# Three pairs of gate/up chunks per FFN in seven block products for both token tiles, with normed rows and an explicit order of steps

## The chip, the core and the metric

One NeuronCore of a Trainium2 chip runs the whole program. The metric is the device time of one execution in microseconds (us), lower is better; the median of the runs of a kernel is compared. Five engines work side by side, each through its own queue in order: the tensor engine (PE; its weight loads are shown apart as PEld), the vector engine (DVE), the scalar engine (ACT), GpSimd (POOL) and the sync engine (SP), which here only issues transfers (DMAs).

## The reference

Two layers, each of three sublayers, on 256 tokens of width 1024 in float32:

```
x = x + 0.5 * rms_norm(swiglu(rms_norm(x, g1), wg, wu, wd), g1post)      # FFN 1
x = x + rms_norm(hybrid_mixer(rms_norm(x, gm), ...), gmpost)             # three attentions, gated
x = x + 0.5 * rms_norm(swiglu(rms_norm(x, g2), wg, wu, wd), g2post)      # FFN 2

def swiglu(x, wg, wu, wd):
    return (jax.nn.silu(x @ wg) * (x @ wu)) @ wd                         # 1024 -> 2816 -> 1024
```

The change is in the four FFNs, in how their weights are prepared, and in what sets the order; the mixers compute as before.

## The kernel before, in words

**Tiles.** The tokens are two tiles of 128, called lanes 0 and 1. All weights lie in one array as 212 half-blocks of 128 x 2048 float32 (1 MB), in the order of their use. An FFN has 11 chunks of 256 columns; a chunk has two half-blocks of gate and up columns side by side (512 columns, four slices of K each) and one half-block for the product down (two slices of K, 1024 columns). An FFN is 33 half-blocks, a mixer 40.

**Precision.** The products run in float32r. `Stream.split` (L74 to L92) makes two float32r parts of each weight, a quarter-block of 128 x 1024 at a time: ACT copies it to `whi` (L88), DVE subtracts to get `wlo` (L89). The inputs are transposed on PE and split likewise (`split_T`, L192 to L199). `mm3` (L240) then takes three matmuls for one product: hi by hi (L245), hi by lo (L247), lo by hi (L250). A half-block with one lane is so 12 matmuls of 512 columns, called a block product here, whether it is of gate/up, of down, or of the mixer.

**Order.** Each lane is a generator that yields after a block product; a list of places (L625 to L645) runs lane 1 `LAG` = 3 half-blocks behind lane 0, so that each half-block of split weights serves both. Six split half-blocks (`W_BUFS`) and three unsplit ones (`RAW_BUFS`) fit. The framework then schedules the traced instructions into one queue for each engine.

**Between sublayers.** `postnorm` (L223) sums the squares of the down product on ACT (L163), takes the power on POOL (L155, L157), scales on DVE (L232) and adds to the residual `x` (L233). `gained` (L207, L211) multiplies by the next gain only, `prenorm` (L213) transposes that (L197), and the reciprocal of the norm is applied later, as a scale of the rows that come out of the products (L303, L305). So PE can begin with a sublayer before its norm is known. Both lanes do this, one about three half-blocks after the other, while PE works for the other lane.

**Names.** In the kernel before, `f010` is layer 0, second FFN, lane 0, and `f011` its lane 1; `m01` is the mixer of layer 0, lane 1. In the kernel after, FFNs are numbered as sublayers: `f20` and `f21` are the same second FFN of layer 0, lanes 0 and 1. `gu` is the sum of a gate/up chunk in PSUM, `acc` that of the product down, `h` the gated product, `hp` and `hT` its transposes.

Of the kernel before, what the change touches and what calls it, by code (L numbers as in the profile page):

```python
# [16 lines left out]
P = 128  # L17
# [28 lines left out]
REST_HEADS, REST_GATE, REST_FFN, REST_FFN_END = 6, 3, 4, 1  # L46
# [8 lines left out]
class Stream:  # L55
    """One half-block of weights after another: loaded, and split into two float32r parts
    whose sum is the float32 weight exactly."""

    def __init__(self, nc, wall, raw, wp):
        self.nc, self.wall, self.raw, self.wp = nc, wall, raw, wp  # L60
        self.raws, self.ready = {}, {}
        self.n = self.loaded = 0

    def load(self, j):
        """Loads run ahead of the splits."""
        while self.loaded < min(j, L * LAYER_BLKS):
            i = self.loaded
            w = self.raws[i] = self.raw.tile([P, BLK], F32, tag="raw", name=f"raw{i}")
            step = HALF if i == 0 else BLK
# [4 lines left out]
    def split(self, n=1):  # L74
        """The next n quarter-blocks."""
        nc = self.nc
        for _ in range(n):
            i, h = divmod(self.n, 2)
            if i == L * LAYER_BLKS:
                return  # L80
            self.load(i + 1)
            if h == 0:
                self.ready[i] = [self.wp.tile([P, BLK], F32R, tag="w" + c, name=f"w{c}{i}")
                                 for c in ("hi", "lo")]
# [3 lines left out]
            nc.scalar.activation(hi, w, AF.Copy)  # L88
            nc.vector.tensor_sub(lo, w, hi.bitcast(F32))  # L89
# [10 lines left out]
def trunk(ctx: ExitStack, tc, x, wall, gpre, gpost, lamv, dgain, cst, out):  # L100
# [5 lines left out]
    ps = ctx.enter_context(tc.tile_pool(name="ps", bufs=2, space=PSUM))  # L106

# [9 lines left out]
    # The tensor engine's clock rises under load only: products of zeros until the inputs are here.  # L117
# [22 lines left out]
    w.load(2)  # L140
    cs = sp.tile([P, C_W], F32, tag="mg", name="cs", bufs=2)
    nc.sync.dma_start(cs, cst)
    lv = sp.tile([P, L, 4, HD], F32, tag="mg", name="lv", bufs=2)
    nc.sync.dma_start(lv, bass.AP(tensor=lamv.tensor, offset=lamv.offset,
                                  ap=[[0, P], [1, L * 4 * HD]]))
    dg = cp.tile([P, L], F32, tag="dg", name="dg")
    nc.sync.dma_start(dg, dgain)
# [40 lines left out]

    def pair(nk, name, tag, bufs):
        return [sp.tile([P, nk, P], F32R, tag=tag + c, name=name + c, bufs=bufs) for c in "hl"]  # L190

    def split_T(src, dst, a, n, name):  # L192
        """Blocks a..a+n of src, [128, 128] each -> their transposes in two float32r parts."""
        hi, lo = (d[:, a:a + n] for d in dst[:2])
        pt = ps.tile([P, 4, P], F32, tag="tr", name=name)
        for k in range(n):
            nc.tensor.transpose(pt[:, k, :], src[:, (a + k) * P:(a + k + 1) * P], ident)  # L197
        nc.scalar.activation(hi, pt[:, :n], AF.Copy)  # L198
        nc.vector.tensor_sub(lo, pt[:, :n], hi.bitcast(F32))  # L199
# [5 lines left out]
    xg = {}  # L205
# [7 lines left out]
    def prenorm(t, i, name):  # L213
        """The gained inputs, transposed, and the reciprocals of their norms."""
        src = xg.pop(t)
        r = rstd_of([sumsq(xs[t], D, name)], D, 1, 1.0, name + "r", "rpre")
        xT = pair(KD, name + "T", "xT", NT)
        for a in (0, 4):
            split_T(src, xT, a, 4, f"{name}p{a}")
        yield  # L220
        return xT, r

    def postnorm(t, acc, i, scale, name):  # L223
        """Adds the normed product to the residual, by halves."""
        y = sp.tile([P, D], F32, tag="t4", name=name + "y", bufs=4)
        r = rstd_of([sumsq(acc[:, c], D // 2, name + str(n)) for n, c in enumerate(HALVES)],
                    D, 1, scale, name + "r")
        g = gain("post", i)
        for c in HALVES:
            if c.start:  # L230
                yield
            nc.vector.scalar_tensor_tensor(y[:, c], acc[:, c], r, g[:, c], op0=ALU.mult, op1=ALU.mult)  # L232
            nc.vector.tensor_add(xs[t][:, c], xs[t][:, c], y[:, c])  # L233
            if i + 1 < 3 * L:
                gained(t, i + 1, c)
            else:
                nc.scalar.dma_start(out[t * P:(t + 1) * P, c], xs[t][:, c])
        yield

    def mm3(o, xT, k, wblk, kk, width, first, last):  # L240
        """o[tokens, width] += x[:, k] @ w[kk], in float32r parts."""
        xh, xl = xT
        wh, wl = (b.rearrange("p (k n) -> p k n", n=width) for b in wblk)
        for n in range(0, width, 512):
            nc.tensor.matmul(o[:, n:n + 512], xh[:, k, :], wh[:, kk, n:n + 512],  # L245
                             start=first, stop=False)
            nc.tensor.matmul(o[:, n:n + 512], xh[:, k, :], wl[:, kk, n:n + 512],  # L247
                             start=False, stop=False)
        for n in range(0, width, 512):
            nc.tensor.matmul(o[:, n:n + 512], xl[:, k, :], wh[:, kk, n:n + 512],  # L250
                             start=False, stop=last)
# [13 lines left out]
    def wide(acc, xT, k0, j, first, last):  # L265
        """Two k of a 1024-wide product; at the end its first half is ready before the second."""
# [14 lines left out]
    def ffn(t, l, which, j):  # L281
        nm = f"f{l}{which}{t}"
        xT, r = yield from prenorm(t, 3 * l + (0 if which == 0 else 2), nm)
        acc = ps.tile([P, D], F32, tag="acc", name=nm + "acc")
        hs = {}

        def down(c):
            finish(hs[c].pop())
            wide(acc, hs.pop(c), 0, jd[c], c == 0, c == NFC - 1)

        ju, jd, n = {}, {}, j
        for c in range(NFC):
            ju[c] = n
            n += 2
            if c:
                jd[c - 1] = n
                n += 1
        jd[NFC - 1] = n
        for c in range(NFC):
            gu = ps.tile([P, 512], F32, tag="gu", name=f"{nm}gu{c}")  # L300
            yield from proj(gu, xT, ju[c], 2)
            s = sp.tile([P, FC], F32, tag="tok", name=f"{nm}s{c}", bufs=4)
            nc.scalar.activation(s, gu[:, :FC], AF.Silu, scale=r)  # L303
            h = sp.tile([P, FC], F32, tag="tok", name=f"{nm}h{c}", bufs=4)
            nc.vector.scalar_tensor_tensor(h, gu[:, FC:], r, s, op0=ALU.mult, op1=ALU.mult)  # L305
            hs[c] = pair(FC // P, f"{nm}hT{c}", "mT", 4)
            hs[c].append(start(split_T_later(h, hs[c], 0, FC // P, f"{nm}hp{c}",
                                            REST_FFN if c < NFC - 1 else REST_FFN_END)))
            yield
            if c:  # L310
                down(c - 1)
                yield
        down(NFC - 1)
        yield from postnorm(t, acc, 3 * l + (0 if which == 0 else 2), 0.5, nm + "o")

# [8 lines left out]
    def constants():  # L324
        """What the mixers need, once."""
# [17 lines left out]
    def rotate(src, t, name):  # L343
        """Partial rotary on [128, 8 heads, 64], in place."""
# [11 lines left out]
    def heads_T(dst, o, t, scale, rot, name, tag, bufs):  # L356
        """A projection in PSUM -> [2 heads x 64, 4 pairs, tokens] in SBUF."""
# [7 lines left out]
        pt = ps.tile([P, 4, P], F32, tag="tr", name=name + "p")  # L365
# [7 lines left out]
    def groups(t):  # L373
        """The eight maps of a mixer in groups whose scores fill two banks."""
# [3 lines left out]
    def softmax(t, mixer, qT, ms, name):  # L378
        """exp(scores - max) [128 q, parity, maps, keys] and the reciprocals of its sums. The
# [351 lines left out]
```

## Time and profile before

| | |
|---|---|
| median of 3 runs | 1301.6 us (1301.24 to 1301.8) |
| span of the profiled execution | 1299.8 us |
| PE busy | 1281.0 us, 99% of the span |
| PEld busy | 1040.9 us |
| DVE busy | 750.9 us, 58% |
| ACT busy | 707.0 us, 54% |
| DMA queue of the weights | 230.28 MB |

The profile is of one execution, whose own span is 1299.8 us from the first to the last instruction; 1.8 us of the median lie around it. Engine times are busy times. Matmuls overlap each other, so a matmul of 0.39 us is followed by the next after 0.23 us, and the spacing of their starts is their price. Rows of the timeline read: start, duration, engine, line of the kernel, operation, output and inputs, shape, count, and in brackets the idle time of that engine just before, with what ended it.

### The profile page before, as it was taken

The numbers are of one execution on the slowest core, as the hardware profiler recorded it, in microseconds if no ns is written. First come the engines' busy times: TensorE is split into PE (matmuls) and PEld (weight loads), VectorE is DVE, ScalarE is ACT, GpSimd is POOL, SyncE is SP. The second block draws the span as 40 slices with busy tenths as digits, with TensorE's granted clock in tenths as the row PEclk, the third lists the DMA queues.
The fourth block names the chain that finished last, engine by engine and source line by source line (L and its number), as shares of the span: only waits on it lengthen the run. The fifth ranks groups of instructions, "written<-read, shape, count | busy, mean of one in ns | idle before, by whom it ended". The sixth has DMA issues, their size and how long they took to land.

```text
span 1299.8 us, 15509 instructions
## 1 busy us (share of the span) xinstructions
PE 1281.0 (99%) x6178; PEld 1040.9 (80%) x6178; DVE 750.9 (58%) x973; ACT 707.0 (54%) x1033; POOL 38.0 (3%) x82
## 2 busy tenths in 40 slices
PE   8999999999999999999999999999999999999997
PEld 5888887888877878888788888788888787788885
DVE  6645457656566675445565545666665666644552
ACT  5545446678575554444554444656976655544441
POOL 0000001000000010000000000100000000000000
PEclk9999999999999999999999999999999999999999
DMA  8845555444534555555555555554344444555530
GB/s 310 309 163 194 187 178 202 147 162 136 188 130 171 185 195 194 193 179 183 190 198 191 194 190 179 181 195 162 130 163 164 160 165 174 196 194 185 179 123 32
DMA packets 34056, 232.37 MB, mean 179 GB/s; under 512 B 3904, under 2 KB 4032, under 8 KB 6976
## 3 DMA queue, kind: packets, MB, share of 16 engines
q1 hardware_dynamic: 33264, 230.28, 50.2%
q8 instruction: 48, 0.79, 0.2%
q10 hardware_dynamic: 720, 1.11, 0.2%
q14 instruction: 24, 0.20, 0.0%
HBM read 230.33 MB, written 1.05 MB: 178 GB/s over the span
## 4 chain that ended last, share of the span: by engine, by line
PE 92%; DVE 3%; ACT 2%; issue 1%; POOL 1%; DMA 1%; SPq 0%; POOLq 0%; DVEq 0%; ACTq 0%
PE f000gu L247 2%; PE f000gu L250 2%; PE f000gu L245 2%; PE f001gu L245 1%; PE f011gu L245 1%; PE f101gu L245 1%; PE f111gu L245 1%; PE f111gu L250 1%; PE f101gu L250 1%; PE f011gu L250 1%; PE f001gu L250 1%; PE f011gu L247 1%; PE f001gu L247 1%; PE f101gu L247 1%; PE f111gu L247 1%; PE f010gu L245 1%
## 5 line engine op out<-in xcount | busy, mean ns | idle before, releaser
L89 DVE TENSOR_TENSOR wlo<-raw,whi 128x1024 fp32r<-128x1024 f32 x424 | 506.4, 1222 | 301.2 <-ACT whi L88 300.8
L88 ACT ACTIVATE whi<-raw 128x1024 fp32r<-128x1024 f32 x424 | 432.0, 1055 | 226.0 <-PE f011gu L250 27.0
L245 PE MATMUL f000gu<-whi,f000Th 128*128 128x512 f32 x88 | 35.3, 401 | 0.8 <-ACT f000Th L198 0.8
L245 PE MATMUL f001gu<-whi,f001Th 128*128 128x512 f32 x88 | 35.1, 399 | 0.2 <-ACT f001Th L198 0.2
L245 PE MATMUL f011gu<-whi,f011Th 128*128 128x512 f32 x88 | 35.3, 401 | 0.0
L247 PE MATMUL f000gu<-wlo,f000Th 128*128 128x512 f32 x88 | 35.0, 398 | 0.3 <-DVE wlo L89 0.3
L245 PE MATMUL f111gu<-whi,f111Th 128*128 128x512 f32 x88 | 35.3, 401 | 0.0
L245 PE MATMUL f101gu<-whi,f101Th 128*128 128x512 f32 x88 | 35.2, 400 | 0.0
L250 PE MATMUL f000gu<-whi,f000Tl 128*128 128x512 f32 x88 | 34.9, 397 | 0.0
L245 PE MATMUL f100gu<-whi,f100Th 128*128 128x512 f32 x88 | 34.5, 392 | 0.0
L245 PE MATMUL f010gu<-whi,f010Th 128*128 128x512 f32 x88 | 34.5, 392 | 0.0
L245 PE MATMUL f110gu<-whi,f110Th 128*128 128x512 f32 x88 | 34.4, 391 | 0.0
L250 PE MATMUL f100gu<-whi,f100Tl 128*128 128x512 f32 x88 | 34.4, 391 | 0.0
L250 PE MATMUL f111gu<-whi,f111Tl 128*128 128x512 f32 x88 | 34.4, 391 | 0.0
L250 PE MATMUL f011gu<-whi,f011Tl 128*128 128x512 f32 x88 | 34.4, 391 | 0.0
L250 PE MATMUL f101gu<-whi,f101Tl 128*128 128x512 f32 x88 | 34.4, 391 | 0.0
L250 PE MATMUL f001gu<-whi,f001Tl 128*128 128x512 f32 x88 | 34.4, 390 | 0.0
L247 PE MATMUL f010gu<-wlo,f010Th 128*128 128x512 f32 x88 | 34.3, 390 | 0.0
L247 PE MATMUL f110gu<-wlo,f110Th 128*128 128x512 f32 x88 | 34.3, 390 | 0.0
L247 PE MATMUL f100gu<-wlo,f100Th 128*128 128x512 f32 x88 | 34.3, 390 | 0.0
L247 PE MATMUL f011gu<-wlo,f011Th 128*128 128x512 f32 x88 | 34.3, 389 | 0.0
L250 PE MATMUL f110gu<-whi,f110Tl 128*128 128x512 f32 x88 | 34.3, 389 | 0.0
(1889 smaller groups left out, 3154.6 us busy)
## 6 DMA issues: line engine op xcount, KB each, us to landing
raw<-wall_dram SPq DMA_DIRECT2D x211, 1024.0 KB, 4.8
gpre<-gpre_dram SPq DMA_DIRECT2D x6, 512.0 KB, 6.2
gpost<-gpost_dram SPq DMA_DIRECT2D x6, 512.0 KB, 4.0
raw<-wall_dram SPq DMA_DIRECT2D x2, 512.0 KB, 7.9
out_dram<-x ACTq DMA_DIRECT2D x4, 256.0 KB, 2.0
x<-x_dram SPq DMA_DIRECT2D x2, 256.0 KB, 3.0
x<-x_dram SPq DMA_DIRECT2D x1, 512.0 KB, 9.1
cs<-cst_dram SPq DMA_DIRECT2D x1, 352.0 KB, 11.5
```

The source lines that it names most:

```text
L88: nc.scalar.activation(hi, w, AF.Copy)
L89: nc.vector.tensor_sub(lo, w, hi.bitcast(F32))
L245: nc.tensor.matmul(o[:, n:n + 512], xh[:, k, :], wh[:, kk, n:n + 512], start=first, stop=False)
L247: nc.tensor.matmul(o[:, n:n + 512], xh[:, k, :], wl[:, kk, n:n + 512], start=False, stop=False)
L250: nc.tensor.matmul(o[:, n:n + 512], xl[:, k, :], wh[:, kk, n:n + 512], start=False, stop=last)
```

## The change

**Seven products.** In each FFN, chunks 1 and 2, 4 and 5, 7 and 8 are taken in pairs. A pair with both lanes and both halves of K is a 2 x 2 by 2 x 2 product of blocks, eight block products before. The kernel after forms it in seven (a scheme of the Strassen kind): two of the seven use a block of the inputs and one of the weights as they are, the others use sums of input blocks, of weight blocks, or of both. Chunks 0, 3, 6, 9 and 10 and all products down stay as they were.

**What the sums cost.** DVE adds weight blocks in place, a quarter-block at a time (`Stream.step`, L134); four of the seven weight items of a pair are such sums, and all seven are split (`recipe`), where four half-blocks were. For each FFN, four sums of input blocks are made once (L408) and split (L410, L411), from float32 copies of the transposes that ACT keeps (L276). The results are put together from three PSUM sums by one ACT copy (L465) and five DVE operations of 128 x 512 for a pair (L468 to L481).

**Norm.** The sums need both lanes on one scale. So in front of an FFN `normed` (L290) computes the norm first and multiplies rows by norm and gain in one step (L296), and only then come the transposes. In front of a mixer it stays as it was.

**Order and room.** `program()` writes out all steps; lane 1's steps follow a pattern of their own in each FFN. Five split half-blocks fit instead of six, five unsplit ones instead of three (the four blocks of a pair stay until their last sum), and the transposes' PSUM has one buffer under each of two tags instead of two under one. At the start of the program ACT and DVE follow the written order for the first five steps. The mixer's lane 1 is four half-blocks behind for the last eight.

```diff
-W_BUFS = 6
-RAW_BUFS = 3
+W_BUFS = 5
+RAW_BUFS = 5
...
+        if isinstance(k, int):
+            return [("split", k, c, (k,) if c else (), 2) for c in range(2)]
+        name, (b11, b12, b21, b22) = k
+        at, plus, free = {"B11": (b11, None, ()), "T1": (b11, b12, ()), "B21": (b21, None, ()),
+                          "T2": (b11, b22, ()), "B22": (b22, None, ()),
+                          "T3": (b12, b22, (b12, b22)), "T4": (b11, b21, (b11, b21))}[name]
...
+            nc.vector.tensor_add(self.raws[op[1]][:, c], self.raws[op[1]][:, c], self.raws[op[2]][:, c])
...
+    def normed(t, i):
+        with soon():
+            r = rstd_of([sumsq(xs[t], D, f"n{i}{t}")], D, 1, 1.0, f"n{i}{t}r", "rpre")
+            xg[t] = sp.tile([P, D], F32, tag="t4", name=f"xg{i}{t}", bufs=4)
+            for c in HALVES:
+                nc.vector.scalar_tensor_tensor(xg[t][:, c], xs[t][:, c], r, gain("pre", i)[:, c],
+                                               op0=ALU.mult, op1=ALU.mult)
...
+            for n, o, x, op, y in (("1", a22, a21, ALU.subtract, a22), ("2", a22, a22, ALU.subtract, a11),
+                                   ("3", a11, a11, ALU.subtract, a21), ("4", a12, a12, ALU.add, a22)):
+                nc.vector.tensor_tensor(o, x, y, op=op)
+                hi, lo = self.S[n] = pair(4, f"{self.nm}S{n}", "k2", 8)
+                nc.scalar.activation(hi, o, AF.Copy)
+                nc.vector.tensor_sub(lo, o, hi.bitcast(F32))
...
+        out = [p(c, "1"), u(0, e, 0), u(0, e, 1), p(c, "5"), p(c, "2")] + more()
+        out += [u(1, e, 0), u(1, e, 1), p(c, "6")] + more() + [p(c, "3")] + more()
+        return out + [p(c, "7")] + more() + [*last[:1], p(c, "4"), *last[1:]]
...
+    if n:
+        out = pre[0] + [u(0, 0, 0), u(0, 0, 1), p(1, "1"), pre[1][0], p(1, "2"), pre[1][1],
+                        u(1, 0, 0), u(1, 0, 1), d(0, 0), p(1, "5"), u(0, 3, 0), u(0, 3, 1), p(1, "6"), p(1, "3"),
+                        d(1, 0), u(1, 3, 0), u(1, 3, 1), p(1, "7"), d(0, 3), p(1, "4"), d(1, 3)]
+        out += seven(4, 6, two(1), (d(0, 6), d(1, 6))) + seven(7, 9, two(4))
```

In the excerpt, `p(c, "5")` is the fifth of the seven products of the pair that begins with chunk c, `u(t, c, hb)` a plain block product of lane t, `d(t, c)` a product down, `pre` the transposes of a lane.

**ACT at the start of the program** (`f000Th` and `f00Th` are lane 0's transposed inputs, `f00q` the copy kept for the sums, `f001j` and `n01j` the sum of squares of lane 1). Before:

```order
L163 ACTIVATE f000j_125,f000s_126<-x0_73 128x1024
L88 ACTIVATE whi0_172<-raw0_102 128x1024
L198 ACTIVATE f000Th_131<-f000p0_133 128x512
L198 ACTIVATE f000Th_131<-f000p4_140 128x512
L88 ACTIVATE whi0_172<-raw0_102 128x1024
L163 ACTIVATE f001j_150,f001s_151<-x1_74 128x1024
L198 ACTIVATE f001Th_156<-f001p0_158 128x512
```

After:

```order
L229 ACTIVATE n00j_121,n00s_122<-x0_73 128x1024
L143 ACTIVATE whi0_134<-raw0_102 128x1024 x2
L273 ACTIVATE f00Th_143<-f00p0_145 128x512
L276 ACTIVATE f00q_142<-f00p0_145 128x512
L273 ACTIVATE f00Th_143<-f00p4_153 128x512
L276 ACTIVATE f00q_142<-f00p4_153 128x512
L229 ACTIVATE n01j_161,n01s_162<-x1_74 128x1024
```

The second quarter-block moved ahead of the transposes, and two copies came in ahead of lane 1's sum of squares.

**DVE where lane 1 goes from the mixer into the second FFN of layer 0** (`m01oy` is the normed product, `xg21` the FFN's input rows). Before:

```order
L232 SCALAR_TENSOR_TENSOR m01oy_3705<-m01acc_3577,m01or_3712,gpost1_3628 128x512
L89 TENSOR_TENSOR wlo78_3743<-raw78_3603,whi78_3742 128x1024
L233 TENSOR_TENSOR x1_74<-x1_74,m01oy_3705 128x512
L232 SCALAR_TENSOR_TENSOR m01oy_3705<-m01acc_3577,m01or_3712,gpost1_3628 128x512
L211 TENSOR_TENSOR xg21_3718<-x1_74,gpre2_3633 128x512
L233 TENSOR_TENSOR x1_74<-x1_74,m01oy_3705 128x512
```

After:

```order
L323 SCALAR_TENSOR_TENSOR m01oy_3744<-m01acc_3644,m01or_3751,gpost1_3632 128x512 x2
L325 TENSOR_TENSOR x1_74<-x1_74,m01oy_3744 128x512
L274 TENSOR_TENSOR f20Tl_3717<-f20p4_3757,f20Th_3716 128x512
L325 TENSOR_TENSOR x1_74<-x1_74,m01oy_3744 128x512
L144 TENSOR_TENSOR wlo86_3806<-raw77_3578,whi86_3805 128x1024 x2
L296 SCALAR_TENSOR_TENSOR xg21_3773<-x1_74,n21r_3770,gpre2_3693 128x512 x2
L134 TENSOR_TENSOR raw75_3496<-raw75_3496,raw78_3642 128x1024
```

The first half of the input rows was made as soon as half of the residual was there; it now stands behind all of the residual, since it takes the norm `n21r`.

**DVE in the middle of the same FFN.** Before, the splits of half-blocks 88 to 90 (chunks 3 to 5):

```order
L89 TENSOR_TENSOR wlo88_4192<-raw88_4077,whi88_4191 128x1024 x2
L305 SCALAR_TENSOR_TENSOR f010h4_4213<-f010gu4_4160,f010r_3670,f010s4_4211 128x256
L89 TENSOR_TENSOR wlo89_4235<-raw89_4120,whi89_4234 128x1024
L199 TENSOR_TENSOR f011hT3l_4190<-f011hp3_4229,f011hT3h_4189 128x256
L89 TENSOR_TENSOR wlo89_4235<-raw89_4120,whi89_4234 128x1024
L199 TENSOR_TENSOR f010hT4l_4216<-f010hp4_4254,f010hT4h_4215 128x256
L89 TENSOR_TENSOR wlo90_4273<-raw90_4158,whi90_4272 128x1024 x2
```

After, in the pair of chunks 4 and 5 (`wlo98` is split from the sum in `raw84`; weight items are numbered anew; `f2c4Z` and `f2c4s1` are sums of the pair):

```order
L134 TENSOR_TENSOR raw84_4066<-raw84_4066,raw87_4133 128x1024
L274 TENSOR_TENSOR f21hT1_4212<-f21hp1_4246,f21hT1_4212 128x256
L134 TENSOR_TENSOR raw84_4066<-raw84_4066,raw87_4133 128x1024
L144 TENSOR_TENSOR wlo98_4228<-raw84_4066,whi98_4227 128x1024
L144 TENSOR_TENSOR wlo99_4254<-raw85_4165,whi99_4253 128x1024
L144 TENSOR_TENSOR wlo98_4228<-raw84_4066,whi98_4227 128x1024
L144 TENSOR_TENSOR wlo99_4254<-raw85_4165,whi99_4253 128x1024
L426 TENSOR_TENSOR f20h6_4292<-f20h6_4292,f20gu6_4267 128x256
L144 TENSOR_TENSOR wlo100_4260<-raw80_4190,whi100_4259 128x1024
L468 TENSOR_TENSOR f2c4s15_4309<-f2c4Z_4296,f2c4s1_4251 128x512
L144 TENSOR_TENSOR wlo100_4260<-raw80_4190,whi100_4259 128x1024
```

Between the splits now stand the sums of weights (L134) and of results (L468).

More of the change, by code (lines that the diff above doesn't have):

```diff
@@ L55, with __init__ @@
 class Stream:
-    def __init__(self, nc, wall, raw, wp):
+    def __init__(self, nc, wall, raw, wp, uses):
         self.nc, self.wall, self.raw, self.wp = nc, wall, raw, wp
[L61 to L67, printed above, removed]
+        self.uses, self.now = uses, 0
+        self.last = {k: n for n, k in enumerate(uses)}
+        self.items = list(dict.fromkeys(k for k in uses if k is not None))
+        self.first = {}
+        for n, k in enumerate(uses):
+            self.first.setdefault(k, n)
+        self.ready, self.raws, self.left = {}, {}, {}
+        self.ops, self.blocks, self.thirds = [], [], {}
+        for k in self.items:
+            if not isinstance(k, int) and "T3" in DMA_SUMS:
+                self.thirds[k[1][1]] = k[1][3]
+            self.ops += [(k, op) for op in self.recipe(k)]
+            for blk in self.loads(k):
+                self.blocks.append(blk)
+        self.done = self.loaded = 0
@@ new lines, in loads, with recipe @@
+    def loads(self, k):
+        if isinstance(k, int):
+            return [k]
+        name, q = k
+        return {"B11": [q[0]], "T1": [q[1], q[3]], "B21": [q[2]]}.get(name, [])
+    def recipe(self, k):
+        if isinstance(k, int):
+            return [("split", k, c, (k,) if c else (), 2) for c in range(2)]
[3 more added lines that the diff above has]
+                          "T3": (b12, b22, (b12, b22)), "T4": (b11, b21, (b11, b21))}[name]
+        ops = [("add", at, plus, c) for c in range(2)] if plus is not None and name not in DMA_SUMS else []
+        ops += [("split", at, c, free if c else (), 2) for c in range(2)]
+        after = {"B11": ("T1", b11, b12), "T1": ("T2", b11, b22), "T2": ("T4", b11, b21)}.get(name)
+        if after and after[0] in DMA_SUMS:
+            ops += [("dma", *after[1:])]
+        return ops
@@ L68, in load @@
+    def load(self, most=RAW_BUFS):
+        while self.loaded < len(self.blocks) and len(self.raws) < most:
+            i = self.blocks[self.loaded]
             w = self.raws[i] = self.raw.tile([P, BLK], F32, tag="raw", name=f"raw{i}")
-            step = HALF if i == 0 else BLK
+            step = HALF if self.loaded == 0 else BLK
             for c in range(0, BLK, step):
@@ L72, in load, with add_by_dma @@
             self.loaded += 1
-    def split(self, n=1):
-        nc = self.nc
[L77 to L83, printed above, removed]
+            if i in self.thirds:
+                self.add_by_dma(i, self.thirds[i])
+    def add_by_dma(self, at, plus):
+        self.nc.gpsimd.dma_start(self.raws[at], self.wall[plus], accum_op=ALU.add)
@@ new lines, in room, with step @@
+    def room(self, k):
+        i = self.items.index(k, max(0, len(self.ready) - 1))
+        return i < W_BUFS or self.last[self.items[i - W_BUFS]] < self.now
+    def step(self):
+        nc = self.nc
+        k, op = self.ops[self.done]
+        self.load()
+        if op[0] == "dma":
+            self.add_by_dma(*op[1:])
+        elif op[0] == "add":
+            c = slice(op[3] * HALF, (op[3] + 1) * HALF)
+            nc.vector.tensor_add(self.raws[op[1]][:, c], self.raws[op[1]][:, c], self.raws[op[2]][:, c])
+        else:
+            _, at, n, free, of = op
+            if k not in self.ready:
+                self.ready[k] = [self.wp.tile([P, BLK], F32R, tag="w" + c, name=f"w{c}{len(self.ready)}")
@@ L94, in get, with ahead @@
-    def get(self, j):
-        self.split(max(0, 2 * (j + 1) - self.n))
-        return self.ready[j]
+            for f in free:
+                del self.raws[f]
+        self.done += 1
+        self.load()
+    def ahead(self, most):
+        while self.done < len(self.ops) and most > 0:
+            k = self.ops[self.done][0]
+            if self.first[k] > self.now + AHEAD or not self.room(k):
+                return
+            self.step()
+            most -= 1
+    def get(self, k):
+        while k not in self.ready or (self.done < len(self.ops) and self.ops[self.done][0] == k):
+            self.step()
+        return self.ready[k]
@@ L136, in trunk @@
     gain("pre", 0)
-    w = Stream(nc, wall, raw, wp)
+    plan = program()
+    w = Stream(nc, wall, raw, wp, [k for _, k in plan if k is not None])
     w.load(1)
     nc.sync.dma_start(xs[1], x[P:, :])
[L140 to L145, printed above, removed]
+    w.load(3)
     dg = cp.tile([P, L], F32, tag="dg", name="dg")
-    nc.sync.dma_start(dg, dgain)
     nhalf = cp.tile([P, 4], F32, tag="nhalf", name="nhalf")
@@ L245, in mm3, with block @@
             nc.tensor.matmul(o[:, n:n + 512], xh[:, k, :], wh[:, kk, n:n + 512],
-                             start=first, stop=False)
+                             start=first, stop=False, **kw)
             nc.tensor.matmul(o[:, n:n + 512], xh[:, k, :], wl[:, kk, n:n + 512],
-                             start=False, stop=False)
+                             start=False, stop=False, **kw)
         for n in range(0, width, 512):
             nc.tensor.matmul(o[:, n:n + 512], xl[:, k, :], wh[:, kk, n:n + 512],
-                             start=False, stop=last)
+                             start=False, stop=last, **kw)
+    def block(o, left, k, first, last):
+        wb = w.get(k)
+        for kk in range(4):
+            mm3(o, left, kk, wb, kk, 512, first and kk == 0, last and kk == 3,
+                skip_group_check=True)
+            if kk % 2:
+                tick()
+        yield
     def proj(o, xT, j, nhb):
@@ L279, in wide @@
             tick()
[L281 to L314, printed above, removed]
@@ L524, in mixer @@
         nm = f"m{l}{t}"
-        xT, r = yield from prenorm(t, 3 * l + 1, nm)
+        pre = prenorm(t, 3 * l + 1, nm)
+        xT, r = next(pre)
+        next(pre)
+        yield
+        next(pre)
+        yield
         rq = sp.tile([P, 2], F32, tag="rq", name=nm + "rq", bufs=2)
@@ L530, in mixer @@
         mT = {}
-        mg = sp.tile([P, D], F32, tag="mg", name=nm + "mg", bufs=2)
+        mg = [sp.tile([P, 512], F32, tag="mg", name=f"{nm}mg{n}", bufs=4) for n in range(2)]
         def gated(mx, j):
@@ L599, in mixer @@
         yield from postnorm(t, acc, 3 * l + 1, 1.0, nm + "o")
-    def tokens(t):
-        for l in range(L):
-            j = l * LAYER_BLKS
-            yield from ffn(t, l, 0, j)
-            yield from mixer(t, l, j + FFN_BLKS)
-            yield from ffn(t, l, 1, j + FFN_BLKS + MIX_BLKS)
-    lanes = [tokens(t) for t in range(NT)]
-    done = [0] * NT
-    def go(t, block=True):
-        waiting[:] = side if block else []
-        if block:
-            done[t] += 1
-            room = 2 * (min(done[0], done[1] - t) + W_BUFS) - w.n
-            w.split(min(room, 2 if w.n - 2 * max(done) < LEAD else 1))
-        next(lanes[t], None)
@@ L644, in trunk, with run @@
-    go(1, False)
+    now = {}
+    gains_of = {}
+    def run(step, k):
+        kind, n, t, *a = step
+        l, sub = divmod(n, 3)
+        if k is not None:
+            waiting[:] = side
+            w.ahead(4)
+        else:
+            waiting[:] = []
+        if n not in now:
+            j = l * LAYER_BLKS + (0, FFN_BLKS, FFN_BLKS + MIX_BLKS)[sub]
+            now[n] = [mixer(t, l, j) for t in range(NT)] if sub == 1 else FFN(n, j)
+        if sub == 1:
+            next(now[n][t], None)
+        else:
+            getattr(now[n], kind)(t, *a, *((k,) if k is not None else ()))
+        if k is not None:
+            w.now += 1
@@ new lines, in trunk, with program @@
+    with tc.manual_schedule(engines={nc.scalar.engine, nc.vector.engine}):
+        normed(0, 0)
+        for _ in range(2):
+            w.step()
+        for n, (step, k) in enumerate(plan[:START]):
+            run(step, k)
+            if n == 1:
+                normed(1, 0)
+    for n, (step, k) in enumerate(plan[START:]):
+        if n == CONSTANTS:
+            constants()
+        run(step, k)
+def program():
+    out = []
+    for n in range(3 * L):
+        l, sub = divmod(n, 3)
+        j = l * LAYER_BLKS + (0, FFN_BLKS, FFN_BLKS + MIX_BLKS)[sub]
+        steps = mixer_steps(n, j) if sub == 1 else ffn_steps(n, j)
+        if n:
+            i = max(i for i, (_, k) in enumerate(out) if k is not None)
+            out.insert(i + 1, steps.pop(1))
+            out.insert(i, steps.pop(0))
+        out += steps
+    return out
```

246 lines of the change are left out of this document (183 added, 63 removed).

## The prediction

> **What bounds the kernel now.** I read the busy times first, then the chain of work that ended last; both stand on the page:
>
> ```profile
> PE 1281.0 (99%) x6178; PEld 1040.9 (80%) x6178; DVE 750.9 (58%) x973; ACT 707.0 (54%) x1033; POOL 38.0 (3%) x82
> ...
> PE 92%; DVE 3%; ACT 2%; issue 1%; POOL 1%; DMA 1%; SPq 0%; POOLq 0%; DVEq 0%; ACTq 0%
> ```
>
> PE works without a pause and is 92% of the chain, so matmuls taken away come off the end, as long as the other engines keep up. How near they are is read by stage. The view of windows has: stretch, its length, then busy time and count of PE, PEld, DVE, ACT, POOL, the granted clock, DMA share and GB/s. The stretches are the program's start, the places where a mixer and then an FFN gives way to the next FFN, and that next one, the first FFN of layer 1, from its head to the same point of its end:
>
> ```profile
> 0.00:14.00 14.00, 9.69 (x31) 4.60 (x32) 4.89 (x8) 6.65 (x10) 1.37 (x9) 0.92 0.86 308
> 451.00:472.00 21.00, 19.66 (x91) 15.59 (x91) 17.10 (x22) 14.79 (x23) 4.31 (x8) 1.00 0.55 201
> 640.00:661.00 21.00, 20.15 (x95) 16.00 (x94) 17.32 (x24) 13.80 (x24) 3.33 (x8) 1.00 0.56 203
> 640.10:828.80 188.70, 187.85 (x854) 153.83 (x853) 104.74 (x126) 89.45 (x127) 4.13 (x10) 1.00 0.54 190
> ```
>
> In an FFN, DVE is busy 104.74 of 188.70 us (56%), ACT 47%, and PE loses 0.85. A boundary loses PE 0.85 (21.00 less 20.15) to 1.34 (21.00 less 19.66). So the bound is PE, with DVE next, far behind.
>
> **What goes: matmuls.** The timeline prices them; these are the first and last of one block product's 12 hi and lo matmuls, lane 0's next to lane 1's:
>
> ```profile
> 522.06 0.39 PE L245 MATMUL f010gu<-whi,f010Th 128*128 128x512 f32 x1
> ...
> 524.78 0.39 PE L245 MATMUL f011gu<-whi,f011Th 128*128 128x512 f32 x1
> ```
>
> 2.72 us for 12 is 0.2267 each. Three pairs in four FFNs save one block product each: 12 x 2.72 = **-32.6**. The order lists 144 matmuls fewer and as many transposes as before, so this part is certain as work; only the waits can eat it.
>
> **What comes: DVE work.** Prices, from groups of instructions and the timeline:
>
> ```profile
> L89 DVE TENSOR_TENSOR wlo<-raw,whi 128x1024 fp32r<-128x1024 f32 x424 | 506.4, 1222 | 301.2 <-ACT whi L88 300.8
> L88 ACT ACTIVATE whi<-raw 128x1024 fp32r<-128x1024 f32 x424 | 432.0, 1055 | 226.0 <-PE f011gu L250 27.0
> ```
>
> ```profile
> 456.37 1.41 DVE L232 SCALAR_TENSOR_TENSOR m00oy<-m00acc,m00or,gpost 128x512 f32<-128x512 f32 x2 [1.66 <-POOL m00or L157]
> 457.70 1.28 DVE L233 TENSOR_TENSOR x<-x,m00oy 128x512 f32<-128x512 f32 x2
> ...
> 519.98 0.42 DVE L199 TENSOR_TENSOR f010hT3l<-f010hp,f010hT3h 128x256 fp32r<-128x256 f32 x1
> 523.36 2.36 DVE L89 TENSOR_TENSOR wlo<-raw,whi 128x1024 fp32r<-128x1024 f32 x2 [2.96 <-ACT whi L88]
> ```
>
> A split of 128x1024 costs 1.18 behind another (2.36 for two), 1.222 by itself. A weight sum (L134) is in no row; nearest are the split, same size, and the two halves of the residual (1.28 for 1024 columns). I take 1.18 and keep 1.28 for the range: 24 sums per FFN make that 2.4 us of DVE. Per FFN, DVE gains 18 splits and 24 sums (42 x 1.18 = 49.6), 19 operations of 128x512 at 0.64 (12.2) and 4 at 0.705 (2.8); those of 256 columns change kind, at the same price. That is 64.6: DVE 104.7 to 169.3 us. PE in an FFN falls by 8.2 to 180.5. DVE would be 94% busy, and its order decides where PE waits. ACT gains 18 copies of 1.055 and 11 of half that size, about 25: 114 us, 63%, not a bound. DMAs stay the same in number (1 MB half-blocks); at the 0.54 share shown they stay hidden.
>
> One rule speaks against me here. The row is the two splits in 2.36 us, 0.08 less than two alone, so a split begins before its predecessor's end. The Trainium skill's page "VectorE: DVE Perf Modes", section "The DRAIN you can't avoid", says that after each DVE operation the next one waits until the pipe is empty, and starts earlier only when it is not held. By that, 0.04 more for each of the 75 and 3 x 35 large operations counted below, 7.2 us, the sum would end near 1292; the row decides, and I stay with 1.18.
>
> **The start: +3.2.** ACT's queue before, and what followed on DVE, POOL and PE:
>
> ```profile
> 9.59 1.06 ACT L88 ACTIVATE whi<-raw 128x1024 fp32r<-128x1024 f32 x1 [4.08 <-DMA raw<-wall_dram]
> ...
> 10.55 1.07 ACT L198 ACTIVATE f000Th<-f000p 128x512 fp32r<-128x512 f32 x2
> ...
> 12.45 1.05 ACT L163 ACTIVATE f001j<-x 128x1024 f32<-128x1024 f32 x1
> ...
> 13.69 0.67 POOL L155 TENSOR_SCALAR f001r<-f001s 128x1 f32<-128x1 f32 x1 [7.28 <-ACT f001j L163]
> ...
> 14.44 1.41 POOL L157 TENSOR_TENSOR f001r<-f001r,nhalf 128x1 f32<-128x1 f32 x1
> ...
> 14.86 1.18 PE L197 MATMUL f001p<-ident,xg 128*128 128x128 f32 x8
> ```
>
> Now the second `whi` quarter goes first (two starts 0.96 apart: 9.59 + 1.92 = 11.5), then four copies of 0.535 (13.65), then lane 1's sum of squares (1.05, and 0.19 until POOL starts: 14.9). POOL takes 2.16 (13.69 to 15.85): 17.05. Before, lane 1's transposes didn't wait for this; now they do, behind the first half of the rows on DVE (0.705, and 0.15 between engines): 18.0 instead of 14.86, +3.15. The 13 products queued ahead begin 1 us later than before and cannot fill it. I take 3.2; if the split queued behind those rows on DVE (1.18) is late for PE too, 4.4; if POOL's second step takes 0.92, as at the later head below, instead of 1.41, 2.7.
>
> **Heads of the three later FFNs: +3.0 (0 to 9).** Now the transposes wait for the whole chain from the last product down. Its pieces, lane 1's at this boundary:
>
> ```profile
> 463.56 0.39 PE L273 MATMUL m01acc<-whi,m01gT1l 128*128 128x512 f32 x1
> ...
> 466.43 0.54 POOL L157 TENSOR_TENSOR m01or<-m01or,nhalf 128x1 f32<-128x1 f32 x1
> ...
> 470.89 0.63 PE L197 MATMUL f011p<-ident,xg 128*128 128x128 f32 x4 [0.83 <-DVE xg L211]
> ...
> 471.44 1.06 ACT L163 ACTIVATE f011j<-x 128x1024 f32<-128x1024 f32 x1 [0.20 <-DVE x L233]
> ...
> 472.96 0.92 POOL L157 TENSOR_TENSOR f011r<-f011r,nhalf 128x1 f32<-128x1 f32 x1
> ```
>
> Last product's end to POOL's end: 463.95 to 466.97, 3.0. The scaling 1.41 and the adds 1.28 (the rows above); sum of squares and its power 2.44 (471.44 to 473.88); first half of the rows 0.705, and 0.15: 9.0 us for lane 0. For lane 1 a `Tl` of 0.64 stands between the adds on DVE: 9.65. The order puts 36 products (8.16) in front of lane 0's transposes and 36 with four transposes (8.7) in front of lane 1's. PE stalls 0.85 + 0.95 = 1.8 to 2.1, where before a boundary lost 0.85 to 1.34: +1.0 each. It is 0 if products in front cover it, and 3 each if the pair of splits gets into the chain. Queued behind the waiting row-scaling on DVE is the first weight sum; ahead of it a pair of splits (2.36) fits into those 2.44 us of ACT and POOL. SP's weight loads now queue behind loads of gains, and a pair holds four of the five unsplit buffers; with DMAs at half load I price that at 0, at most 3 in all.
>
> **DVE late behind the heads: +7.5 (0 to 18).** From lane 1's rows to the split of `wlo98`, the first summed item of the pair 4/5, the order gives DVE 35 operations of 1024 (41.3), 15 of 512 (9.7), 2 of 0.705 and 16 of 256 at 0.42 (6.7): 59.1 us. PE has by then 235 products (53.3), 24 transposes at 0.14 (3.4; what the FFN's 188 us leave over its products) and the stall, 57.6. So DVE is 1.5 late even if never idle; it waits for ACT's copies and for `gu` at times, 1.0 chosen (under 2% of the stretch): 2.5 per head. It is 0 if the products in front come as late themselves, and near 6 with sums at 1.28 (10 of the 35, 1.0) and 5% idle (3.0). Behind this it has room again (134.3 us of DVE against 139.5 of PE up to item 118), so it is paid once per FFN.
>
> **FFN 0: +2.5 (0 to 12).** The same sum up to the second pair: DVE 75 of 1024 (88.5), 19 of 512 (12.2), 32 of 256 (13.4), small ones 2.4: 116.5. PE: 497 products (112.7) and 32 transposes (4.5): 117.2. A margin of 0.7; with DVE idle for 2 to 3% of it, 2.5 late; with 10%, 11 to 12.
>
> **Sum:** 1299.8 - 32.6 + 3.2 + 3.0 + 7.5 + 2.5 = 1283.4 in the span; the 1.8 us between span and median are added: **1285.2**. Five split buffers instead of six show only where a split waits for a slot, for which the trace has no row near the ends of mixers: 0 taken, 3 at most.
>
> **The rivals.**
>
> *The waits hardly show* (0.18). If DVE runs without idling and its queue meets PE's need in time, only the start is paid: 1301.6 - 32.6 + 3.2 = 1272. For it: margins within 2 us. Against: no row has DVE above 82% (17.32 of 21.00).
>
> *DVE becomes the bound in the FFNs* (0.15), the case that ends slower. 169.3 us of DVE fit into the old 188.7 only if it is kept 90% busy; below that every FFN is longer than before. The densest row has 82%, in 21 us. At 87% an FFN takes 194.6, 5.9 more, four times: 1325. For it: in-order queues, single PSUM buffers for a transpose, `wlo` waiting for ACT nearly always (300.8 of 301.2 us of idle time). Against: that idle time has slack in it, since nothing was asked of DVE.
>
> *The clock falls in the new stalls* (0.08). At the start PE is granted 0.92 of the clock over 14 us, and there these two stand three matmuls apart:
>
> ```profile
> 13.15 0.63 PE L245 MATMUL f000gu<-whi,f000Th 128*128 128x512 f32 x1
> ...
> 14.43 0.63 PE L245 MATMUL f000gu<-whi,f000Th 128*128 128x512 f32 x1
> ```
>
> 0.43 each instead of 0.2267. If each of some 7 new stalls put ten to twelve products at that rate, 2.2 us a time, the 15 us bring 1285 to 1301, no change. Against: the 0.83 of idle time at 470.89 left the granted clock of its stretch at 1.00. The Trainium skill's page "TensorE: Matmul & The Clock Gate", section "HAM oscillation — how this bites in real kernels", puts the limit at PE gaps over about 3.4 us; by that rule none of my stalls would do it, and no run here shows one so long.
>
> **How the numbers follow.** 0.2%, 2.6 us, is about what a measurement can tell from no change. My forecast has 0.59, the rivals 0.18, 0.15 and 0.08. The low end takes in the second case, 1271; the high end, 1303, covers waits twice as large as summed (16 more) and the clock's case; outside lies the DVE-bound case. Faster: 0.59 + 0.18 + 0.02 of the clock's case = 0.79; same 0.06; slower 0.15.
>
> **What would show it.** PE's busy time down by some 30; the first product at 12.2 and lane 1's first transposes near 18.0; 1 us of PE idle before each lane's transposes at three heads, released by DVE's scaling of rows; PE waiting for `wlo` in the first two pairs of an FFN and little after; DVE 92% busy in an FFN. I am wrong if PE waits for DVE all through the FFNs (DVE-bound, or sums above 1.28), if matmuls stand 0.43 apart past the start, or if PE loses under 5 us in all.

## The result, and the profile after

The kernel after takes 1277.24 us (median of 4 runs, 1276.48 to 1277.3) against 1301.65 us: a ratio of 0.9815, 95% interval [0.9801, 0.9829]. It is 24.4 us faster; 16.4 were forecast. Run again beside the last three experiments, it took 1277.15 (0.9817, [0.9803, 0.983]).

First the two rows of the page that were read before: the busy times, and the shares of the chain that ended last.

```profile
PE 1249.8 (98%) x6034; PEld 1014.9 (80%) x6034; DVE 984.5 (77%) x1233; ACT 789.1 (62%) x1149; POOL 52.2 (4%) x82
...
PE 90%; DVE 4%; POOL 3%; issue 1%; ACT 1%; DMA 1%; SPq 0%; POOLq 0%; DVEq 0%; ACTq 0%
```

PE is busy 31.2 us less (1281.0 to 1249.8), DVE 233.6 us more, and PE still carries the chain. By stage, from the view of windows (stretch, length, busy time of PE, PEld, DVE, ACT, POOL, granted clock, DMA share, GB/s): the start, the head of the second FFN of layer 0, 40 us inside that FFN, and the whole first FFN of layer 1.

```profile
0.00:14.00 14.00, 8.08 (x29) 3.55 (x30) 4.74 (x6) 5.44 (x8) 1.06 (x8) 0.88 0.85 305
449.00:470.00 21.00, 18.74 (x85) 14.55 (x83) 18.33 (x23) 15.57 (x24) 5.06 (x8) 1.00 0.36 127
...
485.00:525.00 40.00, 40.00 (x183) 32.74 (x182) 39.24 (x48) 26.63 (x36) 0.00 (x0) 1.00 0.56 211
638.70:820.10 181.40, 179.81 (x817) 147.26 (x818) 163.19 (x192) 109.32 (x155) 5.95 (x9) 1.00 0.53 197
```

The third row carries the result: DVE is busy 39.24 of 40 us and PE all 40.00. DVE has next to no idle time left there, and yet it delays nobody: its results are in time. Over the FFN, DVE stands at 90% and PE loses 1.6 us in 181.4. What PE does wait for, from the view of waits (engine, line, who ended the wait: total, times, longest):

```profile
PE f00p L271 <- DVE xg L296: 2.7, 1, 2.7
PE f00gu L339 <- ACT f00Th L273: 1.9, 1, 1.9
PE f31p L271 <- DVE xg L296: 1.3, 1, 1.3
PE f50gu L344 <- DVE f50Tl L274: 1.2, 1, 1.2
PE f20gu L344 <- DVE f20Tl L274: 1.2, 1, 1.2
PE m11p L271 <- DVE xg L288: 1.2, 1, 1.2
...
PE m01p L271 <- DVE xg L288: 1.1, 1, 1.1
PE f20p L271 <- DVE xg L296: 0.9, 1, 0.9
PE f50p L271 <- DVE xg L296: 0.9, 1, 0.9
PE f01gu L344 <- DVE f01Tl L274: 0.7, 1, 0.7
PE f30p L271 <- DVE xg L296: 0.7, 1, 0.7
PE f00gu L341 <- DVE wlo L144: 0.4, 1, 0.4
```

All of it lies at the start and at the heads, those of the mixers (`m01p`, `m11p`) among them. The one wait for a split (`wlo`), 0.4 us, is at 20.82, in the start; behind the heads there is none.

Where the 24.5 us of span went is worked out by cutting the timeline at the same matmul. The kernels differ only by the matmuls that pairs save (36 per FFN), so the 1501st recorded matmul on split weights of the kernel before and the 1465th of the kernel after stand at the same place in the first mixer, and likewise (3901st, 3793rd) in the second:

| us | start, FFN 0, half of mixer 0 | to half of mixer 1 | rest of the span |
|---|---|---|---|
| before | 400.27 | 598.55 | 301.02 |
| after | 396.26 | 585.52 | 293.56 |
| difference | -4.01 | -13.03 | -7.46 |
| matmuls saved | -8.16 | -16.32 | -8.16 |
| given back | 4.15 | 3.29 | 0.70 |

So the saved products do come out, and 8.1 of 32.6 us are given back, about half of it in the first stretch. (The unchanged kernel profiled again, after_again, has 396.40, 585.44 and 293.49: a cut repeats to 0.15 us.)

### The profile page after: what moved, and what is told of

It reads as the page before. It is cut to its first block, busy times and chain, and to the rows that moved or that the text cites. A ratio compares the mean times of both kernels' runs of the same rounds, so it can differ in the third digit from the quotient of the medians.

```text
span 1275.3 us, 15584 instructions
## 1 busy us (share of the span) xinstructions
PE 1249.8 (98%) x6034; PEld 1014.9 (80%) x6034; DVE 984.5 (77%) x1233; ACT 789.1 (62%) x1149; POOL 52.2 (4%) x82
## 4 chain that ended last, share of the span: by engine, by line
PE 90%; DVE 4%; POOL 3%; issue 1%; ACT 1%; DMA 1%; SPq 0%; POOLq 0%; DVEq 0%; ACTq 0%
DVE wlo L144 1%; PE f01gu L344 1%; PE f00acc L339 1%; PE f51gu L339 1%; PE f51gu L344 1%; PE f30acc L339 1%; PE f31gu L339 1%; PE f50acc L339 1%; PE f31gu L344 1%; PE f51acc L339 1%; PE f00acc L341 1%; PE f30acc L341 1%; PE f20acc L341 1%; PE f20acc L344 1%; PE f00acc L344 1%
## 5 line engine op out<-in xcount | busy, mean ns | idle before, releaser
L144 DVE TENSOR_TENSOR wlo<-raw,whi 128x1024 fp32r<-128x1024 f32 x496 | 588.9, 1219 | 101.7 <-ACT whi L143 101.1
L143 ACT ACTIVATE whi<-raw 128x1024 fp32r<-128x1024 f32 x496 | 503.2, 1055 | 170.8 <-DVE raw L134 23.0
L134 DVE TENSOR_TENSOR raw<-raw,raw 128x1024 f32<-128x1024 f32 x96 | 115.6, 1217 | 0.0
L339 PE MATMUL f00gu<-whi,f00Th 128*128 128x512 f32 x40 | 17.2, 430 | 2.1 <-ACT f00Th L273 1.9
L341 PE MATMUL f00gu<-wlo,f00Th 128*128 128x512 f32 x40 | 16.5, 412 | 0.4 <-DVE wlo L144 0.4
L344 PE MATMUL f00gu<-whi,f00Tl 128*128 128x512 f32 x40 | 16.5, 414 | 0.2 <-DVE f00Tl L274 0.2
L339 PE MATMUL f00acc<-whi,f00hT 128*128 128x512 f32 x40 | 16.2, 404 | 0.0
L339 PE MATMUL f20gu<-whi,f20Th 128*128 128x512 f32 x40 | 16.1, 403 | 0.0
L339 PE MATMUL f30gu<-whi,f30Th 128*128 128x512 f32 x40 | 16.1, 403 | 0.0
L339 PE MATMUL f50gu<-whi,f50Th 128*128 128x512 f32 x40 | 16.1, 402 | 0.0
```

What stands on the lines that cost most here:

```text
L134: nc.vector.tensor_add(self.raws[op[1]][:, c], self.raws[op[1]][:, c], self.raws[op[2]][:, c])
```

## The experiments

All are edits of the kernel after; times are medians, ratios to the kernel before on the same chip. The framework schedules the queues anew for each edit, so from the edited place on the order of instructions can change too; where it matters below, it is said.

**no_pairs.** The pairs as eight ordinary products; sums and copies for them are gone. The order of steps is nearly the same: in a pair, the second and the fifth product now stand ahead of two plain ones instead of behind them. The edit in part (the first pair of a later FFN has a case of its own):

```diff
-        return (("seven", n, name, c), (item, (ju[c], ju[c + 1], ju[c] + 1, ju[c + 1] + 1)))
+        return {"1": [u(0, c, 0), u(0, c, 1)], "5": [u(1, c, 0)], "2": [u(1, c, 1)], "6": [u(0, c + 1, 0)],
+                "3": [u(0, c + 1, 1)], "7": [u(1, c + 1, 0)], "4": [u(1, c + 1, 1)]}[name]
...
```

> The kernel after with its pairs taken as eight ordinary block products again; norm in front, order, buffers and start stay. 'Saved products come out whole' (144 matmuls x 0.2267 = 32.6 us, no wait of PE caused by the pairs except those behind the copies for the sums): 1305 to 1310 us, slower than the kernel before by 4 to 8, which is then the price of the norm in front and of the start. 'DVE late behind the heads eats a third of the gain' (the step of the prediction): 1297 to 1301.

Measured: 1305.65 us, 1.0033 [1.0021, 1.0046], inside the first theory's window and clear of the rival's. Cut as above it has 400.42, 600.83 and 301.71: norm in front, fewer buffers and the new order cost 0.15, 2.28 and 0.69 by themselves. (Its start is flattered: the first transposes began at 8.32, 0.88 earlier than in the kernel after, as the gains landed sooner.) By the medians the pairs bring 28.4 of their 32.6. By the cuts they bring 27.6, since the profiled execution of no_pairs was 0.9 below its median; of the 5.0 given back there, 4.0 are in the first stretch.

**no_sums.** DVE's 96 weight sums are left out, so that the summed items hold plain weights: 102 us less of DVE.

```diff
-            nc.vector.tensor_add(self.raws[op[1]][:, c], self.raws[op[1]][:, c], self.raws[op[2]][:, c])
+            pass
```

> The kernel after without the 96 weight sums on DVE (L134 left out, so the summed items hold plain weights): 27 us less DVE per FFN. 'DVE is never late now': no change, 1275 to 1278 us. 'PE waits for late splits behind the heads and in FFN 0' (10 us in the prediction): 1267 to 1270.

Measured: 1276.97 us, 0.9814 [0.98, 0.9827]: 0.3 us less than the kernel after, whose own runs lie 0.8 apart. The same 40 us inside the FFN, from its view of windows:

```profile
485.00:525.00 40.00, 40.00 (x183) 32.83 (x182) 34.29 (x42) 24.93 (x34) 0.00 (x0) 1.00 0.54 193
```

DVE went from 39.24 to 34.29 and PE did not notice. The rival, PE waiting for late splits, falls.

**dve_head and dve_late.** Four more DVE operations of 128x1024 per FFN, near the head or near the end of the three later FFNs (the tuple names the pair's first half-block).

```diff
             nc.vector.tensor_sub(lo, w, hi.bitcast(F32))
+            if not isinstance(k, int) and k[0] in ("T1", "T2") and k[1][0] in (75, 108, 181):     # dve_late: (93, 126, 199)
+                nc.vector.tensor_sub(lo, w, hi.bitcast(F32))
```

> The kernel after with the splits of the two summed items T1 and T2 of the pair of chunks 1 and 2 subtracted twice in the three later FFNs: 4 more DVE operations of 128x1024 (4.6 us) per FFN near its head. 'DVE is just in time there' (split parts ready 0.2 to 0.6 us before their first use at the narrowest place): PE waits for nearly all of it, 3 x 4.1 to 4.4, so about 1290 us (1287 to 1292). 'DVE has slack everywhere': 1277.

> The same 4 more DVE operations per FFN, but in the pair of chunks 7 and 8, where split parts are ready 4 to 8 us ahead of use. 'Only the narrow place behind the head counts': 1277 us (1276 to 1278). 'DVE is the bound of the whole FFN': as dve_head, about 1290.

Measured: dve_head 1292.11 us, 0.9927 [0.9914, 0.9939]; dve_late 1277.12, 0.9815 [0.9802, 0.9829]. dve_head is 0.1 above what the first theory allowed, dve_late is as it said. The same work costs 15 us in one place and nothing in the other. (In dve_late PE's order of instructions is that of the kernel after; in dve_head those of DVE and PE changed behind the heads, so the 15 us are the price of the added operations and of the new order together.) How narrow the first place is can be read in the kernel after, before anything is added. DVE's queue in the last FFN, and PE's first matmul on the split that DVE makes at 1115.62:

```profile
1111.03 0.68 DVE L411 TENSOR_TENSOR f5S2l<-f51q,f5S2h 128x512 fp32r<-128x512 f32 x1
1111.63 0.68 DVE L408 TENSOR_TENSOR f50q<-f50q,f51q 128x512 f32<-128x512 f32 x1
...
1114.49 1.22 DVE L134 TENSOR_TENSOR raw<-raw,raw 128x1024 f32<-128x1024 f32 x1
1115.62 1.22 DVE L144 TENSOR_TENSOR wlo<-raw,whi 128x1024 fp32r<-128x1024 f32 x1
...
1117.36 4.63 DVE L144 TENSOR_TENSOR wlo<-raw,whi 128x1024 fp32r<-128x1024 f32 x4
...
1121.90 0.42 DVE L426 TENSOR_TENSOR f50h<-f50h,f50gu 128x256 f32<-128x256 f32 x1
1122.23 1.22 DVE L144 TENSOR_TENSOR wlo<-raw,whi 128x1024 fp32r<-128x1024 f32 x1
```

```profile
1117.18 0.39 PE L341 MATMUL f50gu<-wlo,f50Th 128*128 128x512 f32 x1
```

The split ends at 1116.84 and is read at 1117.18: 0.34 us in hand; the next one, the first of the four at 1117.36, has 0.2. In the second FFN of layer 0 the smallest such distance is 0.45.

In dve_head the stretch with two FFNs grew by 7.35 (585.52 to 592.87), 3.7 each, below the 4.1 to 4.4 expected; the last FFN alone grew by 7.46. What happened there, from its waits, ACT's timeline and the windows, and PE's timeline after the wait:

```profile
PE f50gu L341 <- ACT whi L143: 4.1, 1, 4.1
```

```profile
1128.33 6.74 ACT L143 ACTIVATE whi<-raw 128x1024 fp32r<-128x1024 f32 x7 [5.50 <-DMA raw<-wall_dram]
```

```profile
1110.00:1129.00 19.00, 15.39 (x70) 12.30 (x68) 17.11 (x24) 6.42 (x12) 0.00 (x0) 0.99 0.16 55
1129.00:1137.00 8.00, 7.10 (x19) 5.35 (x20) 7.58 (x8) 7.37 (x9) 0.00 (x0) 0.60 0.38 131
1137.00:1145.00 8.00, 8.00 (x39) 6.56 (x38) 7.29 (x10) 3.12 (x6) 0.00 (x0) 1.00 0.49 145
```

```profile
1129.44 0.79 PE L341 MATMUL f50gu<-whi,f50Th 128*128 128x512 f32 x1 [4.05 <-ACT whi L143]
...
1134.28 0.63 PE L341 MATMUL f50gu<-whi,f50Th 128*128 128x512 f32 x1
1134.70 0.63 PE L343 MATMUL f50gu<-wlo,f50Th 128*128 128x512 f32 x1
...
1135.50 0.39 PE L341 MATMUL f5c1Y<-whi,f5S2h 128*128 128x512 f32 x1
1135.72 0.39 PE L341 MATMUL f5c1Z<-whi,f5S4h 128*128 128x512 f32 x1
```

Two things beyond the simple sum. First, the next load of weights was issued 0.06 us behind the end of the same DVE split in both kernels, as if it waited for the unsplit buffer that this split frees: at 1109.43 in the kernel after and at 1123.36 in dve_head. The head itself stands 7.57 us later in dve_head, so the load is 6.4 us late. Two of the added operations stand ahead of that split (2.3 us); the rest is DVE's new order, in which more of the sums of input blocks stand ahead of it. ACT's copy then waited 5.50 us for that load, and PE for the copy. Second, after 4.05 us without work, PE's granted clock is 0.60 over the next 8 us: matmuls stand 0.42 apart until 1135.5 and 0.22 after that.

**start_order.** At the start, one split quarter, one transposed half, then the second of each, lane 1's sum of squares, and only then the copies kept for the sums.

```diff
...
-        for _ in range(2):
-            w.step()
         for n, (step, k) in enumerate(plan[:START]):
+            if n < 2:
+                w.step()
             run(step, k)
             if n == 1:
                 normed(1, 0)
+                for o, i in held:                                  # the copies L276, held back
+                    nc.scalar.activation(o, i, AF.Copy)
...
```

> Only the start of the program: one split quarter, one transposed half, then the second quarter and half, lane 1's sum of squares, and only then the two copies for the sums. 'The start costs its order on ACT and DVE': first product near 11.2 instead of 12.44, lane 1's transposes near 16 instead of 19.1: 1274 us (1273 to 1275.5). 'The start waits for its loads or the slower clock': 1277.

Measured: 1273.74 us, 0.979 [0.9777, 0.9804], 3.4 faster than the kernel after and the fastest of all. The start of the kernel after, ACT and PE from the timeline:

```profile
12.44 0.79 PE L339 MATMUL f00gu<-whi,f00Th 128*128 128x512 f32 x1 [1.92 <-ACT f00Th L273]
...
13.79 0.60 ACT L276 ACTIVATE f00q<-f00p 128x512 f32<-128x512 f32 x1 [1.41 <-DVE f00Tl L274]
...
16.13 1.05 ACT L229 ACTIVATE n01j<-x 128x1024 f32<-128x1024 f32 x1
...
19.11 1.29 PE L271 MATMUL f01p<-ident,xg 128*128 128x128 f32 x8 [0.35 <-DVE xg L296]
```

and of start_order:

```profile
11.03 0.79 PE L343 MATMUL f00gu<-whi,f00Th 128*128 128x512 f32 x1 [0.62 <-ACT f00Th L275]
12.30 1.06 ACT L229 ACTIVATE n01j<-x 128x1024 f32<-128x1024 f32 x1
...
16.84 1.44 PE L273 MATMUL f01p<-ident,xg 128*128 128x128 f32 x8
```

The sum of squares comes 3.8 us earlier, lane 1's transposes 2.3 (16 had been expected; the rows were ready at 15.1, but PE was still at lane 0's products ahead of them, 0.43 apart). By the first cut it is 392.92, 3.34 less than the kernel after, and everything behind is the same: most of the start's loss was its order on ACT and DVE, not its loads.

**copy_first and both.** ACT's copy for the sums written ahead of DVE's subtraction in every FFN; and that together with start_order.

```diff
+            if keep is not None:
+                nc.scalar.activation(keep[:, a:a + n], pt[:, :n], AF.Copy)
             nc.vector.tensor_sub(lo, pt[:, :n], hi.bitcast(F32))
-            if keep is not None:
-                nc.scalar.activation(keep[:, a:a + n], pt[:, :n], AF.Copy)
```

> In the transposes of an FFN, ACT's copy for the sums is written ahead of DVE's subtraction instead of behind it. 'ACT's copies that wait for DVE delay the norm chain' (waits of 1.2 to 1.8 us at 459.68 and 465.63, 1.41 at 13.79): lane 1's transposes at the start near 17 instead of 19.1, and 1 to 1.5 us less PE idle time at two or three heads: 1272 us (1270 to 1275). 'The wait only moves to the subtraction': 1277.

> copy_first and start_order together. If the two delays are separate: 3 at the start and 1 to 1.5 at each of two or three heads less than the kernel after, 1271 us (1269 to 1273). If the copies count at the start alone: 1274.

Measured: copy_first 1276.62 us, 0.9814 [0.98, 0.9827]; both 1276.18, 0.9809 [0.9795, 0.9822]. Neither came out as expected. By the cuts, copy_first wins 2.2 at the start (394.05), about what was expected, and loses 1.3 in the stretch that follows (586.83). Together with start_order, in the run named both, 2.4 are lost there (585.71 to 588.08); its four executions lie 2 us apart, and the profiled one is the slowest. The place is the second FFN. SP's issues of the next gains (`gpre`) and of the next weights (`raw`), in the run both:

```profile
466.17 0.33 SPq L202 DMA_DIRECT2D gpre<-gpre_dram  x1
467.31 0.33 SPq L112 DMA_DIRECT2D raw<-wall_dram  x1
```

In start_order the weights are issued first, at 465.13, and the gains at 467.26. ACT's queue and PE in the run both, after that:

```profile
474.23 1.06 ACT L143 ACTIVATE whi<-raw 128x1024 fp32r<-128x1024 f32 x1 [2.71 <-DMA raw<-wall_dram]
475.20 0.58 ACT L275 ACTIVATE f21Th<-f21p 128x512 fp32r<-128x512 f32 x1
```

```profile
475.83 0.50 PE L343 MATMUL f21gu<-whi,f21Th 128*128 128x512 f32 x1 [1.44 <-ACT f21Th L275]
```

The new order put one DVE split behind lane 1's row scaling, and the load of weights follows it: 2.2 us later, and behind the gains instead of ahead of them. The split on ACT then waits 2.71 us for that load, lane 1's transposed half stands behind the split, and PE waits 1.44 for that half: the wait saved at the head returned behind a transfer. (In start_order two splits stand ahead of that half as well, but their load is there in time.) copy_first has the same new order of the two loads. Its 1.3 us do not show as idle time: PE idles 0.5 less in that stretch than in the kernel after, so its matmuls start 1.8 us further apart in sum, which stays open.

**after_again**, the unchanged kernel for that series:

> The kernel after, unchanged, beside the three that follow: 1277 us (1276 to 1278).

Measured: 1277.15 us.

## Why the prediction was right, and where it was wrong

**The matmuls: right.** 32.6 us fewer in PE's work; with everything around them unchanged they were worth 28.4 (no_pairs).

**The heads: right in size, in part by luck.** +3.0 forecast for the norm in front at three heads; no_pairs, with no pairs at all, shows 2.28 + 0.69. But three things lie in these stretches, and the prediction had one of them. PE's waits at the three heads rise by 3.6 from the kernel before to no_pairs (2.98 to 6.61). The heads of the mixers were put at nothing, because their norm did not move; yet the waits `m01p` and `m11p` above, which no_pairs has too, were shorter in the kernel before, so the head of the second mixer costs 0.85 more (that of the first, 0.77 more, lies in the first stretch). And waits for lane 1's last gated product, 0.56 in each FFN, are gone. The three nearly cancel. From the view of waits of the kernel before:

```profile
PE f011hp L197 <- DVE f011h L305: 0.6, 1, 0.6
...
PE m01p L197 <- DVE xg L211: 0.4, 1, 0.4
PE m11p L197 <- DVE xg L211: 0.3, 1, 0.3
```

Why the mixers' heads wait longer, the runs do not show. With pairs the heads and what follows give back 4.0; of the last 1.0, 0.45 is idle time of PE, and the rest stays open. At the FFNs' heads the waits are where they were expected, before the transposes, plus one that was only named as `Tl` and not priced for lane 0: DVE's scaling stood waiting for POOL ahead of lane 0's subtraction,

```profile
462.99 1.41 DVE L323 SCALAR_TENSOR_TENSOR m01oy<-m01acc,m01or,gpost 128x512 f32<-128x512 f32 x2 [1.08 <-POOL m01or L223]
...
464.91 0.68 DVE L274 TENSOR_TENSOR f20Tl<-f20p,f20Th 128x512 fp32r<-128x512 f32 x1
```

and PE lost 1.2 us behind that subtraction in two FFNs.

**The start: mechanism half right.** 3.2 forecast; 4.15 measured over the first stretch, which also holds FFN 0 and the head of the first mixer. The chain through lane 1's norm was the one named. But I priced the four copies on ACT as if they followed each other; the copy for the sums also waits for DVE's subtraction (1.41 at 13.79, 0.76 at 15.64), so lane 1's sum of squares began at 16.13, not 13.65. POOL then took 0.8 instead of the 2.16 summed, which hid half of that: lane 1's transposes came at 19.11, not 18.0. start_order shows that most of the loss, 3.34, was this order and not the norm.

**DVE late behind the heads, +7.5, and FFN 0, +2.5: wrong, both are 0.** This is the step that made the forecast 8 us too high (10.0, less the 1.0 too little at the start and 1.0 at the heads), and no_sums shows it: 102 us less of DVE bring 0.3. The error is in the price. I took PE's matmuls by the spacing of their starts and DVE's operations by their durations, or, for splits, by half of a pair's 2.36, where 2.36 less 1.22 is 1.14. DVE's rows overlap as well: a sum recorded with 1.22 is followed after 1.13 (1114.49 to 1115.62), a 256-wide operation with 0.42 after 0.33 (1121.90 to 1122.23), a 512-wide one with 0.68 after 0.60 (1111.03 to 1111.63). At those prices the stretch from lane 1's rows to `wlo98` sums to 39.6 + 9.0 + 1.3 + 5.3 = 55.2 instead of 59.1. The trace has 56.5, from 469.18 to 525.7, with 0.75 of idle time in it, where I had added 1.0; PE needs the split at 526.9:

```profile
522.21 4.62 DVE L144 TENSOR_TENSOR wlo<-raw,whi 128x1024 fp32r<-128x1024 f32 x4
```

```profile
526.93 0.39 PE L341 MATMUL f2c4Z<-wlo,f2S1h 128*128 128x512 f32 x1
```

The second half of `wlo98` is the third of these four, by the order shown under The change. So DVE is 1.2 early, where 2.5 late had been summed. I had also looked at the wrong place: the narrowest is the pair before, with 0.2 to 0.8 us in hand, which dve_head showed to be real. In FFN 0 the same spacings make 109 of the 116.5 summed for DVE, against PE's 117.2; behind the start the smallest distance there stayed above 5 us.

The rule that was weighed against my price, from the Trainium skill's page "VectorE: DVE Perf Modes", section "The DRAIN you can't avoid", would have moved the sum the wrong way: four splits behind each other take 4.63 here (1117.36), a spacing of 1.14 where one alone is recorded with 1.22, and the row decides.

**The rivals.** The waits-hardly-show case gave 1272, nearer than the forecast; what it missed is the heads. DVE as the bound of the FFNs did not come: where DVE was busy for 98% of 40 us, PE lost nothing. The 82% of the densest row of before, which I had let count against the first rival and for this one, was no limit. The clock rival did not come in this kernel (longest stall behind the start 1.3, granted clock 1.00), but dve_head shows the effect at 4.05. That agrees with the limit of about 3.4 us in the Trainium skill's page "TensorE: Matmul & The Clock Gate", section "HAM oscillation — how this bites in real kernels"; behind the start, stalls between 1.44 and 4.05 are in no run.

## What to carry to other kernels

Price every in-order engine by the spacing of its starts in a dense stretch, not by the durations of its rows; over the 68 operations of the stretch above the difference, 3.9 us, was larger than the margin in question. An engine's busy share doesn't tell whether it is late: look for how long before its use each result is ready, at the narrowest place, since the same four operations in each of three FFNs cost 15 us there and nothing elsewhere. An extra reader of a shared tile, like the copies for the sums, can queue behind another engine; at the start of this program, where nothing covers it, its place in the queue was worth 2.2 us (copy_first), and the whole order there 3.4.

## What the hardware showed that was not expected

An engine can be kept busy for 98% of 40 us by instructions that wait on two other engines and on loads, without one late result; I had counted on some 2% of idle time and on lateness. And a delay on DVE grew on its way: in the last FFN of dve_head, 4.6 us of work cost 7.46, since a load was issued later and PE's matmuls then stood 0.42 apart for 6 us, with a granted clock of 0.60 over 8 us.
